# A copy of overlapping windows: staging eleven and a half batches of 32 through SBUF instead of eleven

## The chip, the cores and the metric

One core of one Trainium2 chip runs the kernel. The metric is the device time of one execution in microseconds (us). Times differ from job to job, and each job ran on one chip: what is compared is from one job unless the text says otherwise. Spans in a profile are about 1.8 us shorter than the time of the same execution.

## The reference

```python
batch, length, dim = (32, 4096, 256)          # float32
window_size, stride = 64, 32
n_windows = (length - window_size) // stride + 1          # 127
for i in range(n_windows):
    result[:, i] = x[:, i*32 : i*32 + 64]
```

There is no arithmetic. A batch of the input is 128 blocks of 32 rows, 32 KB each (4.19 MB); window w of a batch is blocks w and w+1. So every block but the first and the last of a batch is written twice, as the second half of one window and as the first half of the next. 134 MB come in and 266.3 MB go out.

## The kernel before

It mixes two ways of copying. A **direct** copy goes from HBM to HBM: every output byte is read from HBM once and passes the DMA engines once. A **staged** batch is loaded into SBUF (128 partitions, a 32 KB block on each) and stored from there twice, once as first halves and once as second halves: HBM is read half as often, but the DMA engines move the load in addition to the stores, 12.6 MB where a direct batch has 8.3. Batches 1, 4, 7 ... 31 are staged, eleven of them; the other 21 are direct.

```python
def load(self, q, t, b, shift):
    return q.dma_start(out=t[:, :],
        in_=self.xap(b * self.nb - shift, [[self.blk, self.nb], [1, self.blk]]),
        max_dma_last_dim=IN)                     # 16 KB pieces
def store(self, q, t, b, half, shift):
    w = b * self.nw - half - shift
    return q.dma_start(out=self.oap(2 * w + half, [[2 * self.blk, self.nb], [1, self.blk]]),
        in_=t[:, :], max_dma_last_dim=OUT)
...
staged = [*range(1, B, 3)]
direct = [b for b in range(B) if b not in staged]
...
with tc.tile_critical():
    st.run(ring_s)                               # ACT queue: 6 loads, 12 stores, 5 loads, 10 stores
    for b in direct:                             # SP queue: 7 x 16 windows of each direct batch
        ...
        for j in range(7):
            todo -= 1
            sem = near if todo == 2 else done    # third from last direct copy
            share += 90 if turns % (loads + per * stores) < loads else 12
            if share >= 120:                     # split: first halves, then second halves
                share -= 120; turns += 4
                count(c.windows(ring_d, b, w, 16, 0), done)
                count(c.windows(ring_d, b, w, 16, 1), sem)
            else:
                turns += 3
                count(c.windows(ring_d, b, w, 16), sem)
            w += 16
    ring_r.wait_ge(near, 16)                     # POOL queue: the 15 windows left of each
    ...                                          # direct batch, after the stores beside them
    st.wait_stored(ring_d, len(staged) - 1)
    count(c.columns(ring_d, last, 125, 2), done) # repairs what the last store overwrote
```

A store of 128 blocks writes one half window too many at an end of its batch, into a window of the neighbouring batch; a direct copy repairs it afterwards (the "edges", on the POOL queue, and the last small copy on the SP queue). A direct copy of 16 windows that is split takes four turns per DMA engine (two 32 KB packets and two semaphore writes), an unsplit one three; so the rate of splitting sets how many direct bytes pass between the staged packets. And the POOL queue takes over from the SP queue when the signal `near` arrives.

## Time and profile before

| | kernel before |
|---|---|
| time, 6 runs beside the changed kernel | 752.64 us median (751.67 to 753.82) |
| bytes on the DMA engines | 313.26 MB |
| HBM read, written | 220.95, 267.09 MB |
| staged, direct, edges | 138.41, 154.32, 20.51 MB |

The lines of its page: the busy share of the 16 DMA engines in 40 slices of the span (in tenths), the rate in each slice, the queues (q1 is the SP queue, q10 ACT, q0 POOL: packets, MB, share of the time of 16 engines), and the HBM traffic.

```profile
span 743.6 us, 309 instructions
...
DMA  9999999999999999999999999999999999999995
GB/s 369 430 429 433 433 437 428 425 422 434 422 420 419 438 423 414 431 428 423 423 431 413 424 427 436 432 426 428 433 425 433 423 427 432 423 426 436 423 428 241
...
q1 hardware_dynamic: 7952, 154.32, 48.9%
q10 hardware_dynamic: 8976, 138.41, 43.9%
q0 software_dynamic: 1168, 20.51, 6.5%
...
HBM read 220.95 MB, written 267.09 MB: 656 GB/s over the span
```

The engines are full from the second slice to the last but one. The three shares sum to 99.3%. Nothing computes, so time is bytes divided by the engines' rate, if the packets run at their best.

Whether they do is read from the trace's packet records, each with a size and a duration. The median 32 KB packet takes 1213 ns and the median 16 KB packet 611 ns, 27.0 and 26.8 bytes per ns; sixteen engines at that rate are 432 GB/s. I price every packet at the median of its size in this trace, sum, and divide by 16: 729.5 us per engine. What the packets really took is 8.6 us more. I call that surplus **stretch**. What is left of the span (743.6 - 729.5 - 8.6 = 5.5 us) I call start and end. It is a net figure: by the packet records the engines idle about 2.1 us in the first 25 us and 7.2 in the last 40, and in between the records overlap a little (a share of 1.01), which takes 3.8 off. These three terms are used for every trace below, always at the same medians.

The end of the execution, from the timeline (start and length in us, engine, line, what):

```profile
647.41 10.25 POOL L34 DMA_DIRECT2D out_dram<-in_x_dram  x18 [646.97 <-DMA out_dram<-in_x_dram]
697.42 1.72 POOL L34 DMA_DIRECT2D out_dram<-in_x_dram  x3 [39.75 <-DMA out_dram<-xb]
699.13 0.58 POOL L44 DMA_DIRECT2D out_dram<-in_x_dram  x1
738.18 0.58 SPq L44 DMA_DIRECT2D out_dram<-in_x_dram  x1
```

POOL starts its edges at 647 us, waits once for a staged store, and the small repair copy of the SP queue is issued at 738.18, after the last store has landed.

### The profile page before, as it was taken

What the parts mean: (1) busy time and instruction counts of PE and PEld (TensorE: products, weight loads), DVE (VectorE), ACT (ScalarE), POOL (GpSimd) and SP (SyncE); (2) the same over time, 40 slices, a digit from 0 to 9 for tenths busy, and PEclk for the clock granted to TensorE, in tenths of its full rate; (3) what the DMA queues carried; (4) which work ended last, traced back from release to release, by engine and by line L of the source; (5) the groups of instructions that cost most, each with busy time, mean ns of one, the idle gap of its engine ahead of it and who ended that gap; (6) DMA issues with size and microseconds to landing.
All of it is one profiled execution on the core that took longest, in us unless ns stands there. A gap on an engine that the chain in (4) does not pass through costs nothing.

```text
span 743.6 us, 309 instructions
## 1 busy us (share of the span) xinstructions
POOL 12.8 (2%) x26
## 2 busy tenths in 40 slices
POOL 0000000000000000000000000000000000130100
DMA  9999999999999999999999999999999999999995
GB/s 369 430 429 433 433 437 428 425 422 434 422 420 419 438 423 414 431 428 423 423 431 413 424 427 436 432 426 428 433 425 433 423 427 432 423 426 436 423 428 241
DMA packets 18098, 313.26 MB, mean 421 GB/s; under 512 B 4144, under 2 KB 4144, under 8 KB 4336
## 3 DMA queue, kind: packets, MB, share of 16 engines
q1 hardware_dynamic: 7952, 154.32, 48.9%
q10 hardware_dynamic: 8976, 138.41, 43.9%
q0 software_dynamic: 1168, 20.51, 6.5%
q14 instruction: 2, 0.02, 0.0%
HBM read 220.95 MB, written 267.09 MB: 656 GB/s over the span
## 4 chain that ended last, share of the span: by engine, by line
another core or an unknown queue 92%; POOL 2%; issue 0%; POOLq 0%; SPq 0%
POOL out_dram L34 2%; POOL out_dram L44 0%; POOLq L214 0%; SPq L141 0%; POOLq L94 0%
## 5 line engine op out<-in xcount | busy, mean ns | idle before, releaser
L34 POOL DMA_DIRECT2D out_dram<-in_x_dram x21 | 12.0, 576 | 686.7 <-DMA out_dram<-in_x_dram 647.0
L44 POOL DMA_DIRECT2D out_dram<-in_x_dram x1 | 0.6, 581 | 0.0
L200 POOL MEMSET const-float32-0.0<- 128x1 f32 x1 | 0.1, 99 | 0.2 <-issue 0.2
L200 POOL MEMSET const-bfloat16-1.0<- 128x1 bf16 x1 | 0.1, 102 | 0.0
L200 POOL MEMSET const-float32-1.0<- 128x1 f32 x1 | 0.1, 99 | 0.0
L200 POOL MEMSET const-uint8-127<- 128x1 uint8 x1 | 0.1, 99 | 0.0
## 6 DMA issues: line engine op xcount, KB each, us to landing
out_dram<-in_x_dram SPq DMA_DIRECT2D x96, 1024.0 KB, 100.8
out_dram<-xb ACTq DMA_DIRECT2D x22, 4096.0 KB, 142.5
out_dram<-in_x_dram SPq DMA_DIRECT2D x102, 512.0 KB, 89.1
xb<-in_x_dram ACTq DMA_DIRECT2D x11, 4096.0 KB, 122.0
out_dram<-in_x_dram POOLq DMA_DIRECT2D x20, 960.0 KB, 37.8
out_dram<-in_x_dram POOLq DMA_DIRECT2D x1, 576.0 KB, 40.3
out_dram<-in_x_dram POOLq DMA_DIRECT2D x1, 256.0 KB, 36.8
out_dram<-in_x_dram SPq DMA_DIRECT2D x1, 128.0 KB, 2.5
```

The lines of the kernel that those rows point to most:

```text
L34: return q.dma_start(out=self.oap((b * self.nw + w0) * 2 + h, [[2 * blk, n], row]), in_=self.xap(b * self.nb + w0 + h, [[blk, n], row]), m ...
L44: return q.dma_start(out=self.oap((b * self.nw + w0) * 2, [[part, 16], [2 * self.blk, n], row]), in_=self.xap(b * self.nb + w0, [[part, 16 ...
L200: nc = _bacc.Bacc("TRN2", target_bir_lowering=False, num_devices=1)
```

## The change

The intent: HBM, not only the engines, seems to limit the mix, so let a little more of it pass through SBUF. The first half of batch 0 (64 blocks, on every second partition so that its bytes spread over SBUF) becomes a twelfth staged item, the seventh in order. The rate at which direct copies are split is set anew so that direct and staged work take equally many turns. The edges are listed anew, and three single half windows are copied by themselves in the middle of the run, where before had one. Core of the diff, with cuts marked:

```diff
-    def load(self, q, t, b, shift):
+    def load(self, q, t, b, c, n):
         return q.dma_start(
-            out=t[:, :],
-            in_=self.xap(b * self.nb - shift, [[self.blk, self.nb], [1, self.blk]]),
+            out=t[:: 128 // n, :],
+            in_=self.xap(b * self.nb + c, [[self.blk, n], [1, self.blk]]),
 ...                                              (store likewise)
+    items = [(b, -1 if b == B - 1 else 0, c.nb) for b in staged]
+    items.insert(6, (0, 1, c.nb // 2))
 ...
-            for j in range(7):
-                todo -= 1
-                sem = near if todo == 2 else done
-                share += 90 if turns % (loads + per * stores) < loads else 12
+        for i, (b, w) in enumerate(sixteens):
+            sem = near if i == len(sixteens) - 2 else done
+            loading = turns < first_loads or 0 <= turns - first_loads - stores < loads
+            share += 108 if loading else 51
 ...
+    edges = [(b, 0 if b - 1 in staged else 112, 15) for b in direct[1:-1]] + [(0, 113, 14)]
 ...
-        count(c.columns(ring_r, last, 116, 9), rest)
-        st.wait_stored(ring_d, len(staged) - 1)
+        count(c.columns(ring_r, last, 117, 8), rest)
+        st.wait_stored(ring_d, place[B - 1])
         count(c.columns(ring_d, last, 125, 2), done)
```

More of the change, by code (lines that the diff above doesn't have):

```diff
@@ L47, in columns, with store @@
         )
-    def load(self, q, t, b, shift):
+    def load(self, q, t, b, c, n):
         return q.dma_start(
-            out=t[:, :],
-            in_=self.xap(b * self.nb - shift, [[self.blk, self.nb], [1, self.blk]]),
+            out=t[:: 128 // n, :],
+            in_=self.xap(b * self.nb + c, [[self.blk, n], [1, self.blk]]),
             max_dma_last_dim=IN,
         )
-    def store(self, q, t, b, half, shift):
-        w = b * self.nw - half - shift
+    def store(self, q, t, b, c, n, half):
+        w = b * self.nw + c - half
         return q.dma_start(
-            out=self.oap(2 * w + half, [[2 * self.blk, self.nb], [1, self.blk]]),
-            in_=t[:, :],
+            out=self.oap(2 * w + half, [[2 * self.blk, n], [1, self.blk]]),
+            in_=t[:: 128 // n, :],
             max_dma_last_dim=OUT,
@@ L68, with __init__ @@
 class Staging:
-    def __init__(self, c, tc, pool, dtype, batches, bufs, shifts):
-        self.c, self.batches, self.shifts = c, batches, shifts
+    def __init__(self, c, tc, pool, dtype, items, bufs):
+        self.c, self.items = c, items
         self.tiles = [pool.tile([128, c.blk], dtype, name=f"xb{i}") for i in range(bufs)]
@@ L75, in __init__ @@
         self.stored = [tc.alloc_semaphore(f"stored{i}") for i in range(bufs)]
-    def shift(self, g):
-        return self.shifts.get(self.batches[g], 0)
     def load(self, q, g):
@@ L83, in load @@
             q.wait_ge(self.stored[i], 32 * n)
-        self.c.load(q, self.tiles[i], self.batches[g], self.shift(g)).then_inc(self.loaded[i], 16)
+        self.c.load(q, self.tiles[i], *self.items[g]).then_inc(self.loaded[i], 16)
     def store(self, q, g):
@@ L89, in store @@
         for half in (0, 1):
-            self.c.store(q, self.tiles[i], self.batches[g], half, self.shift(g)).then_inc(self.stored[i], 16)
+            self.c.store(q, self.tiles[i], *self.items[g], half).then_inc(self.stored[i], 16)
     def wait_stored(self, q, g):
@@ L97, in run @@
         bufs = len(self.tiles)
-        for first in range(0, len(self.batches), bufs):
-            group = range(first, min(first + bufs, len(self.batches)))
+        for first in range(0, len(self.items), bufs):
+            group = range(first, min(first + bufs, len(self.items)))
             for g in group:
@@ L121 @@
     staged = [*range(1, B, 3)]
+    items = [(b, -1 if b == B - 1 else 0, c.nb) for b in staged]
+    items.insert(6, (0, 1, c.nb // 2))
+    place = {b: g for g, (b, _, n) in enumerate(items) if n == c.nb}
     direct = [b for b in range(B) if b not in staged]
     pool = ctx.enter_context(tc.tile_pool(name="xb", bufs=1))
-    st = Staging(c, tc, pool, x.dtype, staged, 6, {0: -1, B - 1: 1})
+    st = Staging(c, tc, pool, x.dtype, items, 6)
     ring_d, ring_s, ring_r = nc.sync, nc.scalar, nc.gpsimd
@@ L136, in count @@
         total[sem] += 16
-    per, loads, stores = 6, 6 * 17, 34
-    todo = 7 * len(direct)
+    sixteens = []
+    for b in direct:
+        w = c.nb // 2 + 1 if b == 0 else 15 if b - 1 in staged else 0
+        sixteens += [(b, w + 16 * j) for j in range((c.nw - w) // 16)]
+    singles = [(0, 0, 0), (0, c.nb // 2, 1), (B - 1, c.nw - 1, 1)]
+    edges = [(b, 0 if b - 1 in staged else 112, 15) for b in direct[1:-1]] + [(0, 113, 14)]
+    last = B - 2
+    edges.append((last, 112, 5))
+    first_loads, loads, stores = 6 * 17, 5 * 17 + 9, 6 * 34
     turns = share = 0
@@ L142 @@
         st.run(ring_s)
-        for b in direct:
-            w = 0 if b - 1 not in staged else 8 if b + 1 in staged and b + 1 < B - 1 else 15
-            for j in range(7):
-                todo -= 1
-                sem = near if todo == 2 else done
-                share += 90 if turns % (loads + per * stores) < loads else 12
-                if share >= 120:
-                    share -= 120
-                    turns += 4
-                    count(c.windows(ring_d, b, w, 16, 0), done)
-                    count(c.windows(ring_d, b, w, 16, 1), sem)
-                else:
-                    turns += 3
-                    count(c.windows(ring_d, b, w, 16), sem)
-                w += 16
-                if todo == 7:
-                    count(c.windows(ring_d, B - 1, c.nw - 1, 1, 1, 2048), done)
-                    if 0 in staged:
-                        count(c.windows(ring_d, 0, 0, 1, 0, 2048), done)
@@ L164 @@
-        ring_r.wait_ge(near, 16)
-        pieces = (32768,)
-        last = B - 2
-        for i, b in enumerate(direct[:-1]):
-            for g, n in enumerate(staged):
-                if abs(n - b) == 1:
-                    st.wait_stored(ring_r, g)
-            parts = [(0, 15)] if b - 1 in staged else [(112, 15)]
-            if b - 1 in staged and b + 1 in staged:
-                parts = [(0, 8), (120, 7)]
-            for w, n in parts:
-                count(c.windows(ring_r, b, w, n, None, pieces[i % len(pieces)]), rest)
@@ L178 @@
-        count(c.windows(ring_r, last, 112, 4), rest)
-        count(c.columns(ring_r, last, 116, 9), rest)
-        st.wait_stored(ring_d, len(staged) - 1)
+        for i, (b, w) in enumerate(sixteens):
+            sem = near if i == len(sixteens) - 2 else done
+            loading = turns < first_loads or 0 <= turns - first_loads - stores < loads
+            share += 108 if loading else 51
+            if share >= 120:
+                share -= 120
+                turns += 4
+                count(c.windows(ring_d, b, w, 16, 0), done)
+                count(c.windows(ring_d, b, w, 16, 1), sem)
+            else:
+                turns += 3
+                count(c.windows(ring_d, b, w, 16), sem)
+            if i == len(sixteens) // 2:
+                for b, w, half in singles:
+                    count(c.windows(ring_d, b, w, 1, half, 2048), done)
@@ L181 @@
+        ring_r.wait_ge(near, 16)
+        for b, w, n in edges:
+            for k in (b - 1, b + 1):
+                if k in place and b != last:
+                    st.wait_stored(ring_r, place[k])
+            count(c.windows(ring_r, b, w, n), rest)
+        count(c.columns(ring_r, last, 117, 8), rest)
+        st.wait_stored(ring_d, place[B - 1])
         count(c.columns(ring_d, last, 125, 2), done)
```

## The prediction

> **What bounds the kernel now.** It is all DMA. The page's slice rows show the 16 DMA engines at 9 tenths in every slice but the last; the table of windows gives a share near 1.0 from 18.6 us to about 730 us at 424 to 433 GB/s. The queue table splits 313.26 MB into 154.32 (direct, HBM to HBM, SP queue), 138.41 (staged: load 4 MiB, store 8 MiB per batch, ACT queue) and 20.51 (edges, POOL queue). In the trace's packet records a 32 KB packet takes 1213 ns at the median and a 16 KB packet 611 ns, 27.0 and 26.8 bytes per ns, whichever kind it is. At these medians all packets take 729.5 us per engine; longer packets add 8.6 us; about 5.5 us of the 743.6 us span are ramp and tail. So the limit is the engines' byte rate, with a small second limit on top. The Trainium skill, "DMA: Bandwidth & Descriptors", Specifications, gives a fabric ceiling of 435 GB/s; the trace agrees (427 in the steady part).
>
> The 8.6 us of stretch lie mostly in the store stretches: there direct copies carry about 58% of the bytes and packets average 1.5% over their median; in load stretches they carry 54% and the stretch is 0.3%. Direct bytes load HBM twice, staged ones once, so I read this as HBM starting to saturate (the page: 656 GB/s).
>
> **What the change does.**
> 1. Adds a 2.1 MB load and turns 4.2 MB of direct copies into SBUF stores: 313.26 becomes about 315.35 MB: +5.0 us, all critical, since every engine is always busy.
> 2. HBM reads fall by 2.1 MB.
> 3. Splits more direct copies into single-half DMAs: 85 of 143 instead of 51 of 147. The same page, "Queues, rings and completion order", says engines round-robin between queue rows at packet granularity; the shares above fit one packet per turn. In turns per engine (packets plus semaphore writes), direct plus edges is 570 against 561 staged before, about 590 against 588 after, so both sides still end together. The direct share becomes about 0.52 to 0.53 in loads and 0.55 to 0.56 in stores (estimates from the counts), near the shares where before shows 1.003 to 1.007 of stretch. Estimated gain: about 1% of some 375 us of store time, 3 to 5 us.
> 4. Tail unchanged: the last small copy of 2.5 us after the last staged store; POOL has backlog enough.
> 5. Risk: the half batch sits on every second partition, 4 rows per engine; engines may collide at SBUF. 24 data packets of 611 ns per engine: half of them doubled would be +7 us; I expect below 1 us.
>
> **Sum.** 753.6 + 5.0 - 4 - 0.5 (smoother edges) = about 754: gain and cost nearly cancel. Predicted 753.8 us, 8 in 10 between 749.5 and 757.5. Chances: faster by over 2% 0.01, within 2% 0.97, slower by over 2% 0.02.
>
> **What would show each step.** (1) Page: about 315.3 MB, ACT queue 144.7, SP queue 150; packets at medians 734.5 us per engine. (2) HBM read about 2.1 MB lower. (3) Direct share in the store stretches 0.55 to 0.56, total stretch 4 to 5 us instead of 8.6. (4) The last slice near 240 GB/s as before. (5) The half batch's 16 KB packets at 611 ns; if well above, step 5 was wrong.
>
> **What would make it wrong.** If the stretch comes not from the direct share but from something else, it stays: 757 to 758. If it vanishes altogether, about 749. If turns are uneven and one queue runs out early, direct-only traffic at the end would cost several us.

## The result

| | before | changed |
|---|---|---|
| time, 6 runs each | 752.64 us (751.67 to 753.82) | 753.00 us (752.29 to 753.88) |
| ratio changed to before | | 1.0004, 95% interval 0.9991 to 1.0017 |

Ratios here and below are the mean time of one kernel's fast runs over the mean of the other's fast runs of the same rounds, so they are not quite the ratio of the medians quoted.

The same lines of the page of the changed kernel:

```profile
span 752.1 us, 344 instructions
...
DMA  9999999999999999999999999999999999999995
GB/s 369 431 429 429 418 430 426 436 425 426 425 431 420 435 421 430 430 425 426 432 405 417 430 431 430 426 435 429 424 422 428 428 424 428 424 430 424 426 424 192
...
q1 hardware_dynamic: 8368, 150.19, 47.0%
q10 hardware_dynamic: 9408, 144.71, 45.5%
q0 software_dynamic: 1152, 20.45, 6.6%
...
HBM read 218.86 MB, written 267.09 MB: 646 GB/s over the span
```

The bytes moved as planned: 315.36 MB, 6.3 MB more on the ACT queue, 4.1 MB less on the SP queue, 2.1 MB less read from HBM. But the span is 752.1 us, 8.5 above the trace of before, and the last slice carries 192 GB/s instead of 241. Taken at face value the two pages say that the change costs 8.5 us, which the times beside each other deny. The end of the changed kernel:

```profile
656.88 9.88 POOL L34 DMA_DIRECT2D out_dram<-in_x_dram  x17 [656.44 <-DMA out_dram<-in_x_dram]
702.99 2.30 POOL L34 DMA_DIRECT2D out_dram<-in_x_dram  x4 [36.22 <-DMA out_dram<-xb]
705.29 0.54 POOL L44 DMA_DIRECT2D out_dram<-in_x_dram  x1
746.68 0.60 SPq L44 DMA_DIRECT2D out_dram<-in_x_dram  x1
```

In my terms this trace has 734.8 us at medians, 10.5 of stretch and 6.8 at start and end. The first trace of before had 729.5, 8.6 and 5.5. The stretch had not fallen to 4 or 5 us as predicted; it stood higher. So either the mechanism was wrong, or the two traces could not be compared. (This trace and the first one of before need not be from one chip.)

### The profile page after: what moved, and what is told of

Same layout as the page of the kernel before. It is cut to its first block, busy times and chain, and to the rows that moved or that the text cites. A ratio compares the mean times of both kernels' runs of the same rounds, so it can differ in the third digit from the quotient of the medians.

```text
span 752.1 us, 344 instructions
## 1 busy us (share of the span) xinstructions
POOL 12.9 (2%) x26
## 2 busy tenths in 40 slices
DMA packets 18930, 315.36 MB, mean 419 GB/s; under 512 B 4704, under 2 KB 4704, under 8 KB 4912
## 4 chain that ended last, share of the span: by engine, by line
another core or an unknown queue 92%; POOL 2%; issue 0%; POOLq 0%; SPq 0%
POOL out_dram L34 2%; POOL out_dram L44 0%; POOLq L212 0%; SPq L150 0%; POOLq L91 0%
```

## The experiments

All kernels below gave the correct result. There were three jobs, each on one chip: chip A (kernel before 753.14 us median there), chip B (745.55) and chip C (745.53). No chip had two jobs, so what I call a difference of chips could also be one of the jobs. My theory A: the added bytes cost about 5 us, and less stretch, from a lower share of direct bytes, gives it back. The main rival, B: the stretch has nothing to do with that share, and the gain comes from the two ends.

### The kernel before, again (before_again, chip A)

No edit.

> The kernel before, unchanged, for a second trace from one chip together with the next three. Its first trace has a span of 743.6 us while its times lie at 751.7 to 753.8 us, so that trace may be of an untypically short execution. Theory A (the change trades 5 us of bytes against less stretch): the typical trace has a span near 751 us and the packets' stretch over their medians (32 KB 1213 ns, 16 KB 611 ns) is then about 14 to 17 us per engine, not 8.6. Theory B (stretch has nothing to do with it, gain is in ramp and tail): stretch again near 8.6 us and the missing 8 us sit at the two ends. Ratio to before 1.000 within 0.2%: it shows the noise.

Measured: 752.31 us, ratio 0.9997 (0.9968 to 1.0027). From its page:

```profile
span 749.6 us, 309 instructions
...
DMA packets 18098, 313.26 MB, mean 418 GB/s; under 512 B 4144, under 2 KB 4144, under 8 KB 4336
```

The span is 749.6 us, with the same 18098 packets: 729.5 at medians, **15.5** of stretch, 4.6 at the ends. Theory A's expectation holds: on such a chip the kernel before has nearly twice the stretch of its first trace. The first trace is like chips B and C, where the kernel is 7.6 us faster with no change in its instructions.

### The changed kernel, again (after_again, chip A)

No edit.

> The changed kernel, unchanged. Ratio to before 0.999 to 1.002. Theory A: stretch per engine 4 to 6 us below that of the before trace of this chip, packets at medians 734.8 us against 729.5 us. Theory B: the same stretch, 5 us less of ramp and tail.

Measured: 753.88 us, ratio 1.0014 (0.9987 to 1.0042). From its page:

```profile
span 750.9 us, 344 instructions
...
DMA packets 18930, 315.36 MB, mean 420 GB/s; under 512 B 4704, under 2 KB 4704, under 8 KB 4912
```

On one chip, span 750.9: 734.8 at medians (+5.3), 9.8 of stretch (-5.7), 6.4 at the ends (+1.8). The sum is +1.4, and the spans differ by 1.3. Rival B falls: stretch pays for the bytes, and the ends got worse, not better. Of the 5.7 us, 3.1 are saved between 125 and 350 us and 1.6 between 510 and 700, the two store stretches; after 700 us the stretch grew, from 0.5 to 1.8. Each term is from one trace of each kernel; the changed kernel's first trace, whose span is also of the slow kind, has 0.7 more stretch.

Where the stretch fell is read from the DMA view of a store stretch, 150 to 350 us, of the kernel before and then of the changed kernel:

```profile
DMA packets 4612, 84.38 MB, mean 422 GB/s; under 512 B 949, under 2 KB 949, under 8 KB 949
...
q1 hardware_dynamic: 2307, 48.73, 57.9%
q10 hardware_dynamic: 2305, 35.65, 42.7%
```

```profile
DMA packets 5032, 85.51 MB, mean 428 GB/s; under 512 B 1193, under 2 KB 1193, under 8 KB 1241
...
q1 hardware_dynamic: 2519, 46.70, 54.9%
q10 hardware_dynamic: 2513, 38.81, 45.7%
```

The packets of the two queues alternate almost one for one in both (2307 against 2305, 2519 against 2513), as a round robin by packet would give. What changed is the bytes of a turn: the direct queue carries 48.73 of 84.38 MB, 57.7%, before, and 46.70 of 85.51, 54.6%, after. In these windows the packets take 1.0238 times their medians before and 1.0099 after. It is not the direct packets alone that stretch: before, the staged ones stand at 1.026 and the direct ones at 1.022 (in the first trace of before at 1.008 and 1.021). In a load stretch, 430 to 500 us, the reading is less firm: the direct share went from 53.3% to 52.1% and the durations from 1.0082 to 1.0009 of the medians, but the next two kernels have 1.0025 at 53.1% (after_coarse) and 1.0061 at 52.0% (before_fine) there.

### Half batch, old rate of splitting (after_coarse, chip A)

```diff
-            share += 108 if loading else 51
+            share += 90 if loading else 12
```

> The changed kernel with the old rate of splitting the direct copies (47 of 143 split instead of 85), so the extra half batch without the new split rate. Turns per engine then are about 557 direct and edges against 588 staged, so the direct side ends about 31 turns early and the staged queue runs on alone for some 15 to 20 us. Theory A: the direct share in the store stretches stays at 0.58 and the stretch there at that of before; bytes still cost 5 us: ratio 1.003 to 1.006. Theory B (the split rate does not matter): ratio 1.000 as with the change.

Measured: 758.75 us, ratio 1.0079 (1.0048 to 1.0111), above the 1.003 to 1.006 expected. Terms: 734.5 at medians, 16.9 of stretch, 6.0 at the ends, span 757.4. The half batch without the new splitting keeps the stretch of before (the direct share from 150 to 350 us is 56.8%, packets at 1.0273) and pays the bytes on top. That is theory A, and rival B's 1.000 is excluded. The half batch without the new splitting is a loss of nearly 0.8% here; of the 7.8 us by which its span exceeds that of before_again, 1.4 are at the ends, where the queues no longer finish together.

### Eleven batches, new rate of splitting (before_fine, chip A)

```diff
-                share += 90 if turns % (loads + per * stores) < loads else 12
+                share += 108 if turns % (loads + per * stores) < loads else 51
```

> The kernel before with the new rate of splitting (about 87 of 147 split instead of 51), eleven staged batches. Turns per engine about 606 direct and edges against 561 staged, so the staged queue ends early and direct copies run alone for the last 40 to 50 turns. Theory A: stretch in the bulk as low as in the changed kernel, but a direct-only end where both sides of each packet load HBM and packets of 32 KB take 1.2 times their median or more: net ratio 1.003 to 1.012. Theory B (split rate and HBM both without effect): ratio 1.000 and no stretched packets at the end.

Measured: 754.07 us, ratio 1.0016 (0.9990 to 1.0043); the point is below the range expected, which the interval overlaps. Its stretches of time (start:end, length, POOL busy, clock, share of the DMA engines, GB/s):

```profile
100.00:600.00 500.00, 0.00 (x0) 1.00 1.00 426
722.00:740.00 18.00, 0.00 (x0) 1.00 0.99 324
```

Both halves of the expectation show. The direct share from 150 to 350 us is 55.5% and packets there take 1.0142 times their medians instead of 1.0238; on the SP and ACT queues together the stretch is 10.0 us instead of 14.7. Then the staged queue runs out, and from 722 to 740 us, with direct copies alone, the engines are as busy as before (0.99) and move 324 GB/s instead of 426; the edges have 7.8 us of stretch instead of 0.9. So the rate of splitting changes the stretch without any change of the bytes. That it does so through the share of direct bytes is my reading: no run moves the share by more than a point at a fixed rate of splitting, so an effect of the split copies themselves is not excluded. With the ratio at 1.0016, against 1.0014 for the changed kernel, the half batch's bytes cost about as much as the direct-only end that they avoid.

### No staging (direct_only, chip B)

```diff
-    staged = [*range(1, B, 3)]
+    # all 32 batches: 7 x 16 windows on the SP queue, 15 on the POOL queue
 ...                                              (a comment of mine stands for the new loops)
```

> No staging at all: every window goes HBM to HBM, 266.3 MB on the DMA engines instead of 313, about 532 MB of HBM traffic. Theory A (HBM saturates not far above the traffic of before): the time is set by HBM, 750 to 800 us, and 32 KB packets take about 1.25 times 1213 ns. Rival (only the engines' byte rate binds and the stretch is noise): 266.3 MB at 432 GB/s, about 617 us plus 10, packets at 1213 ns.

Measured: 804.73 us, two runs, ratio 1.0794 (1.0775 to 1.0814), a little above the range I gave. From its page:

```profile
DMA packets 12290, 266.37 MB, mean 332 GB/s; under 512 B 4160, under 2 KB 4160, under 8 KB 4160
...
HBM read 266.34 MB, written 266.34 MB: 664 GB/s over the span
```

At medians its packets would take 618.6 us; they take 795.4, 1.29 times as long. The engines are full (share 1.00 from 100 to 600 us) and move 335 GB/s, so HBM reads and writes 670 GB/s together. In the store window of the kernel before on chip A, direct bytes counted twice and staged ones once give an estimate of (2 x 48.73 + 35.65) / 200 us = 666 GB/s, and 661 for the changed kernel. On the fast kind the same count gives 672 GB/s for the first trace of before, 664 for after_third and 655 for twelve (both below). So before is already at the traffic that direct copies alone reach. That HBM is the limit is inferred from these totals. It is not that one queue alone is slow: from 50 to 150 us the SP and the POOL queue run side by side at 333 GB/s, later the SP queue alone at 335. The rival that only the engines bind (627 us) is excluded.

### Half batch on partitions 0 to 63 (contiguous, chip B)

```diff
-            out=t[:: 128 // n, :],
+            out=t[:n, :],                         (and the same in store)
```

> The changed kernel with the half batch on partitions 0 to 63 instead of every second partition. If the spread matters, [...]the half batch's 16 KB packets (24 per engine) stand above 611 ns, up to twice for those that meet, and the time rises by 1 to 7 us (ratio 1.001 to 1.009). If it does not matter because the other queue takes every second turn, ratio equal to that of the change within 0.1%.

Measured: 748.97 us, ratio 1.0045 (1.0032 to 1.0059). The changed kernel was not in this job; on chip C, where the kernel before takes the same time, its ratio is 1.0046 (below). The stretches of time around the load of the half batch, which lands at 396.6 us here and at 395.1 in the changed kernel (its stores, the first that wait for it, are issued then); first this kernel, then the changed one on chip C:

```profile
361.00:381.00 20.00, 0.00 (x0) 1.00 1.00 424
381.00:401.00 20.00, 0.00 (x0) 1.00 1.01 377
401.00:421.00 20.00, 0.00 (x0) 1.00 1.00 429
```

```profile
361.00:381.00 20.00, 0.00 (x0) 1.00 1.01 427
381.00:401.00 20.00, 0.00 (x0) 1.00 1.01 424
401.00:421.00 20.00, 0.00 (x0) 1.00 0.99 424
```

Here the engines are as busy in the middle stretch but move 377 GB/s instead of 424. The load does collide: from 378 to 398 us the packets of the staged queue take 1.29 times their medians, against 1.05 with every second partition. That 1.05 is not the half batch's: half_last, which loads a whole batch at this time, has 1.04. The half batch's stores, about 500 to 520 us, are hardly touched (1.007 against 1.000). The Trainium skill, "SBUF — State Buffer", section "Door 1: The DMA port swizzle", says that bandwidth depends on how many of 16 ports the partitions reach; by its formula partitions 0 to 63 reach eight and every second partition all. The measurement of the load agrees in direction. But the whole trace has 6.3 us of stretch against 5.1, and the time shows nothing. One possible reason, only argued, is that slowing the staged queue also mended its early end. Since two chips are compared, I leave the size open.

### Half batch last (half_last, chip B)

```diff
-    items.insert(6, (0, 1, c.nb // 2))
+    items.append((0, 1, c.nb // 2))
 ...
+        st.wait_stored(ring_d, len(items) - 1)
         for sem in (done, near, rest):
```

> The changed kernel with the half batch as the last staged item instead of the seventh. It writes no window outside its own, so nothing needs to be repaired after it, and the repair after batch 31 (the last small copy of the sync queue) happens while the half batch is still stored. Expected: the 3 to 5 us at the end, in which only that small copy runs, vanish: ratio 0.993 to 0.997. If the end is set by something else (landing of the last direct copies), ratio as with the change, 1.000.

Measured: 747.17 us, ratio 1.0023 (1.0009 to 1.0037), outside the 0.993 to 0.997 expected. The repair copy was indeed issued at 718 us, long before the end, but start and end still take 6.0 us: the repair copy is not what sets the end. By the packet records the last store of the ACT queue lands by 734.1 us on fifteen engines and at 740.6 on the sixteenth, and that engine's last edge pieces follow until 741.8. That expectation failed.

### Twelve batches staged (twelve, chip B)

The first half of batch 3 shares the half batch's tile, on the odd partitions; splits at 120 in loads and 89 in stores. One line of the diff:

```diff
-    items.insert(6, (0, 1, c.nb // 2))
+    items.insert(6, [(0, 1, c.nb // 2), (3, 1, c.nb // 2)])
```

> Twelve staged batches: the first halves of batches 0 and 3 share one tile, on even and odd partitions; splitting raised so that turns stay even (about 615 staged, about 610 direct and edges). Bytes on the engines 317.4 MB: packets at medians about 740 us per engine, 10 us above before. Theory A: the direct share falls to about 0.51 to 0.53 and the stretch by a further 3 to 5 us, so the ratio is 1.000 to 1.004: a flat optimum. Rival (stretch does not depend on the direct share): ratio about 1.005 above that of the change.

Measured: 751.94 us, ratio 1.0087 (1.0073 to 1.0101), above the flat optimum that I expected. 740.1 us at medians, but the stretch is only 3.1: its direct share from 150 to 350 us is 51.8% and the packets there take 1.0004 times their medians. The time alone is near what the rival foretold (0.4% above the changed kernel, whose ratio is 1.0046 on chip C, where it said about 0.5%); the stretch tells them apart. Once the stretch is gone, further staging is pure cost.

### The changed kernel on a third chip (after_third, chip C)

No edit.

> The changed kernel, unchanged, for same-chip comparison with the next three. The two chips met so far differ: before takes about 753 us on one (15.5 us of stretch per engine) and about 745.5 on the other. If this is the slow kind: ratio 0.999 to 1.002; on the fast kind the stretch to be saved is only about 8.6 us, so the bytes (5.3 us) outweigh the gain and the ratio should be 1.002 to 1.005.

Measured: 748.57 us against 745.53, ratio **1.0046** (1.0030 to 1.0062). On this chip the change is a small but clear loss, as the expectation for the fast kind said. Its stretch is 5.1 us. The first trace of before, which is of a chip of this kind, has 8.6, so about 3.5 us are saved (across chips) against 5.3 of bytes.

### Hand-over signal one copy earlier (early, chip C)

```diff
-            sem = near if i == len(sixteens) - 2 else done
+            sem = near if i == len(sixteens) - 3 else done
```

> The changed kernel with the hand-over signal to the edges' queue on the third from last direct copy, as in the kernel before, instead of the second from last. In the changed kernel's traces the staged queue then runs alone for about 4 us (no direct bytes between the last bulk copy and the first edge copy) and so finishes early, leaving direct-only traffic for the last 6 to 8 us at 1.2 times the median packet. Expected: the 4 us gap goes, the end's stretched packets fall, time 0.5 to 2 us below the changed kernel of the same chip (ratio 0.001 to 0.003 lower). If the hand-over is harmless, ratio equal within 0.1%.

This is a piece of the change that I had overlooked when I predicted. Queue lines of the 4 us from 653 to 657 us, first the changed kernel on chip C, then this one:

```profile
q10 hardware_dynamic: 85, 1.39, 81.2%
q0 software_dynamic: 16, 0.49, 28.4%
q1 hardware_dynamic: 4, 0.03, 1.9%
```

```profile
q0 software_dynamic: 39, 0.79, 45.7%
q10 hardware_dynamic: 46, 0.75, 43.9%
q1 hardware_dynamic: 2, 0.03, 1.9%
```

With the later signal, the SP queue has run dry and the edges have hardly begun: 1.39 MB of staged bytes against 0.49 of edges, where the earlier signal gives 0.75 and 0.79. The staged queue gets ahead there. Stretch from 40 to 6 us before the end is 1.0 us in the changed kernel and 0.4 here; on chip A it was 0.4 before and 1.4 after the change. Measured: 747.74 us, ratio 1.0031 (1.0019 to 1.0043), 0.0015 below the changed kernel, but the intervals overlap and the two spans agree to 0.1 us. The gap is shown; its cost, about 1 us by the two ratios, is not resolved. The earlier signal does not shorten the ends: its terms are 4.1 of stretch and 6.7 at start and end, against 5.1 and 5.9 in the changed kernel. In both, one engine ends its part of the last store about 4 us after the other fifteen (739.8 against 736.0 us here, 739.9 against 735.3 in the changed kernel).

### Early signal and half batch last (early_last, chip C)

The two edits together.

> Early signal, and the half batch as the last staged item, so that the repair copy after batch 31 is no longer alone at the end. Expected: a further 1 to 3 us below early, ratio to before 0.997 to 1.001 depending on the chip. If half batch last gives nothing, equal to early.

Measured: 746.54 us, ratio 1.0012 (0.9999 to 1.0025). It is clear of the changed kernel (1.0030 to 1.0062) and level with before, but 1.2 us below early with overlapping intervals, and just above the 0.997 to 1.001 expected. Start and end take 5.7 us instead of 5.9, stretch 4.3 instead of 5.1. It was run on the fast kind of chip only. On chip A, taking its 0.0034 from the changed kernel's 1.0014 gives an estimate of 0.998; that was not run.

### An eighth of a batch last (tiny_last, chip C)

With the early signal; cut to the lines that set the amount and the splitting.

```diff
-    items.append((0, 1, c.nb // 2))
+    items.append((0, 1, 16))
 ...
-            share += 108 if loading else 51
+            share += 96 if loading else 27
```

> Eleven staged batches and, as the last staged item, only 16 rows of batch 0 (an eighth of a batch in place of a half), early signal, 61 of 146 direct copies split so that turns stay even (570 staged, about 577 direct). Bytes on the engines 313.8 MB, 1.3 us above before instead of 5.3; stretch near that of before; the repair copy off the end as in early_last. Expected ratio 0.995 to 0.999, the fastest of all on a fast chip. If the stretch on a slow chip matters more than bytes, early_last wins there.

Measured: 747.55 us, ratio 1.0029 (1.0014 to 1.0043): a miss. It saves 3.9 us at medians against the half batch (730.9), but the stretch is 8.1 and the runs spread from 746.2 to 749.7. At 55.9% direct bytes the packets from 150 to 350 us take 1.0112 times their medians. No version that I ran beats the kernel before clear of noise.

### Direct share and stretch, in one place

Worked out from each trace, 150 to 350 us: direct MB over all MB, and the sum of packet durations over the same packets at their medians. In brackets the number of batches staged.

```
                                    direct share   durations / medians   stretch of the whole trace
chip A  after_coarse (11.5)            56.8%            1.0273                16.9 us
        before_again (11)              57.7%            1.0238                15.5
        before_fine  (11)              55.5%            1.0142                17.8 (7.8 of it in the edges)
        after_again  (11.5)            54.6%            1.0099                 9.8
chips   direct_only  (0)              100.0%            1.2896               176.8
B, C    first trace of before (11)     57.8%            1.0153                 8.6
        tiny_last    (11.1)            55.9%            1.0112                 8.1
        after_third  (11.5)            54.6%            1.0044                 5.1
        twelve       (12)              51.8%            1.0004                 3.1
```

(The chip of the first trace is not on record; its span agrees with chips B and C. The first trace of the changed kernel, of the slow kind by its span, has 54.6%, 1.0112 and 10.5; the four variants with the half batch that are left out, on chips B and C at 54.4 to 54.5%, have 1.0021 to 1.0037.) At the same share, chip A has more stretch than the others. Within each kind the stretch falls with the share, but for the two highest shares of chip A, which differ by 0.9 points. The rate of splitting orders the kernels the same way, so the table alone does not tell the two apart.

## Why the prediction was right, and where its steps were not

The time was right: 753.8 predicted, 753.0 measured. Point by point:

- **What bounds it: right.** The engines' byte rate, with HBM close behind. The Trainium skill, "DMA: Bandwidth & Descriptors", section "Specifications", gives 435 GB/s as the fabric ceiling on the SBUF side; from 150 to 350 us the mixes move 420 to 432. That HBM is the second limit is inferred from the kernel without staging and the end of before_fine.
- **The bytes: right.** +5.0 us predicted, +5.3 at medians (734.8 against 734.5 predicted), 315.36 MB as predicted.
- **The direct share: right.** 0.55 to 0.56 in stores and 0.52 to 0.53 in loads predicted, 0.546 and 0.521 in the windows shown. The same page, "Queues, rings and completion order", describes a round robin by packet, and the counts of the two queues agree.
- **The gain in stretch: right in kind, mis-sized.** "Total stretch 4 to 5 us instead of 8.6" failed: the changed kernel's trace has 10.5. The 8.6 was read from a trace of one kind of chip and added to times from another. On chip A the term is 15.5 to 9.8, a gain of 5.7 where I said 4; on the fast kind it is about 3.5.
- **The ends: wrong.** "Tail unchanged", "both sides still end together" and "smoother edges, 0.5" are not what the traces show. The signal moved one copy, for about 4 us the staged queue ran almost alone, and stretch near the end rose from 0.4 to 1.4 us on chip A. Start and end grew from 4.6 to 6.4 us there, and the last slice is at 192 GB/s, not near 240. The signal does not explain that growth, since the earlier one left start and end as long (early). What the records show is one late engine: in after_again the last store lands by 739.7 us on fifteen engines and at 745.0 on the sixteenth (743.1 and 743.7 in before_again), and the repair copy waits for it. Why it is late stays open.
- **Colliding partitions: right.** Every second partition costs little; contiguous ones do collide.

So on chip A the terms are +5.3 - 5.7 + 1.8 where I wrote +5.0 - 4 - 0.5. Two errors of opposite sign, 1.7 too little gain and 2.3 too little loss at the ends, nearly cancelled: that the point came so close, with a stretch read on one kind of chip and a time on another, was luck. On chip C the ratio of 1.0046, about 3.4 us, is 2.9 us above my sum of +0.5: how the exchange of bytes for stretch comes out differs between the jobs.

## What to carry to other kernels

When two limits stand close together, moving work from one to the other pays only while the second still stretches the work of the first: price the packets at their undisturbed duration, and the surplus is all that can be won. Before two traces are compared, compare their spans with the times, since an 8 us difference here came with the job and its chip and not with the kernel. When the order of a queue is rewritten, check every signal to another queue: one copy later can leave one of them alone for some microseconds.

## What the Trainium skill lacked or had wrong

- "HBM Reference", section "Specifications (TRN2)", says that a core streaming alone is bounded by its 16 DMA engines at about 425 GB/s. It has no figure for copies from HBM to HBM: there the engines stayed full but were held to 335 GB/s, 670 GB/s of reads and writes together, with packets at 1.29 times their best duration.
- "DMA: Bandwidth & Descriptors", section "Latency and other measured facts", calls 214 GB/s per direction full rate for HBM to HBM copies of tiles with a given row pitch. The direct copies here, in contiguous 32 KB packets on the SP queue, ran at 335 GB/s, read and written at that rate each.
- No page that I read says how far one kernel differs from chip to chip at full load: this one took 753.1 us in the job on one chip and 745.5 in the jobs on two others, with 15.5 us of stretch in the one trace and 8.6 in one of the faster kind.
- The same DMA page's "Queues, rings and completion order" speaks of packets of typically 9 to 17 descriptors between turns. Here the turns fit single records of 32 and 16 KB (2307 against 2305 in 200 us); how many descriptors a record holds, the trace does not say.
